# Convolution taps in S5: tables loaded six blocks ahead instead of three, and one more ScalarE copy per block

## The chip, the cores and the metric

The kernel runs on one core of one Trainium2 chip. The metric is the device time of one execution in microseconds (us). TensorE (PE) multiplies into PSUM banks, VectorE (DVE) and ScalarE (ACT) compute on SBUF and PSUM, SyncE (SP) issues nearly all DMAs of this kernel, each engine in the order of its own instruction list.

## What is computed

A two-layer encoder trunk on 512 tokens of width 2048. The change lies in layer 0, whose input projection feeds grouped-query attention and a bidirectional S5 layer:

```
h @ w_in -> q, k, v, g_a, u, g_b
o_a = gqa_block_attention(q, k, v) * silu(g_a)
o_b = s5_mixer(u, ...) * silu(g_b)      # scan of both directions, Re(C h) + D u, GLU
x   = x + gate * (concat([o_a, o_b]) @ w_out)
```

The kernel does S5 in blocks of eight tokens. A short convolution inside a block uses "taps" (products of C, powers of the state matrix, and B); a scan over the 64 blocks carries the state between blocks.

## The kernel before

Projections are units of float32 matmuls, each split into three (lines 167 to 169 with 512 columns, 234 to 236 with 256). Every weight piece of 128x1024 is loaded into a tile `w` (two buffers, L142), rounded by ACT into `wh` (L128) and subtracted by DVE into `wl` (L129); `wh` and `wl` have three buffers. Here "split" means the L129 instruction. In the stretch of interest the projection units use two PSUM banks in turn (`nmain = 2`).

A gate unit (ga0, ga1, ... of g_a) is emptied by `gate_evict`: ACT takes a tanh into the tile `r2k` (L890), DVE multiplies (L891), SP stores it (L892). `r2k` has one buffer, so the next L890 waits until the store before it has landed, and the bank of a unit is free only after its L891.

The S5 work is a background stream that runs between these units. After `s5_in` come, step by step together, `s5_scan` and `s5_kernels`; then comes `s5_out`.

- `s5_scan` is 62 steps on DVE alone, five instructions each (L483 twice, L484, L486 twice), each step needing the one before.
- `s5_kernels` makes the taps of 16 blocks. A block's table `ck` (512 KB) is read from the scratch tensor `s5_ck` (L414), 16 small matmuls (L521; the trace has two records for each) fill two banks, ACT copies them out (L528, L529), DVE adds to 16 columns (L530, and L532, which reads the second bank), SP stores the taps (L533). Three `ck` tiles are in use in turn, `G14` to `G16`, and `G17` holds the copied-out taps.
- `s5_out` reads the taps back in small pieces (L552), copies scan states (L559, L560: these need the whole scan), and multiplies (L570, L573).

The order on each engine is fixed when the program is built: a list scheduler places an instruction when its operands are ready, by its own estimate of time, and by priority, with weights first. On the chip each engine follows that order.

Of the kernel before, what the change touches and what calls it, by code (L numbers as in the profile page):

```python
# [13 lines left out]
ALU = mybir.AluOpType  # L14
# [52 lines left out]
class Trunk:  # L67
# [434 lines left out]
    def s5_kernels(self, ts):  # L502


        nc, A = self.nc, self.A
        self.s5_kk = self.scratch("s5_kk", [16, 128, 240])
        dd = self.sl("s5dd", [128, 2, 16])
        nc.sync.dma_start(out=dd[:, 0], in_=A["s5_dcol"])
        nc.sync.dma_start(out=dd[:, 1], in_=A["s5_dmask"])
        w = self.sl(ts[3], [128, 4, 240])  # L510
        cks = {i: self.s5_load_ck(ts[i], i) for i in range(3)}
        yield
        for i in range(16):
            ck = cks.pop(i)
            kv = [self.bank(f"b{2 * (i % 2) + d}", (128, 128)) for d in range(2)]
            for c in range(2):
                for g in range(4):
                    b0 = (i * 4 + g) // 2 * 32
                    for d in range(2):
                        r = slice(64 * d, 64 * d + 64)  # L520
                        nc.tensor.matmul(out=kv[d][32 * g:32 * g + 32], lhsT=self.s5_bb[c][r, b0:b0 + 32],  # L521
                                         rhs=ck[r, c, g], start=(c == 0), stop=(c == 1),
                                         tile_position=(64 * d, 32 * g))
            if i + 3 < 16:
                cks[i + 3] = self.s5_load_ck(ts[i % 3], i + 3)
            yield
            ks = w[:, i % 4]
            nc.scalar.copy(out=ks[:, 0:128], in_=kv[1])  # L528
            nc.scalar.copy(out=ks[:, 128:240], in_=kv[0][:, 16:128])  # L529
            nc.vector.scalar_tensor_tensor(out=ks[:, 112:128], in0=dd[:, 1], scalar=dd[:, 0, i:i + 1],  # L530
                                           in1=ks[:, 112:128], op0=ALU.mult, op1=ALU.add)
            nc.vector.tensor_tensor(out=ks[:, 112:128], in0=ks[:, 112:128], in1=kv[0][:, 0:16], op=ALU.add)  # L532
            nc.sync.dma_start(out=self.s5_kk[i], in_=ks)  # L533
            yield

# [389 lines left out]
    def layer0(self):  # L925
        nc, A = self.nc, self.A
        G = [f"G{i}" for i in range(18)]
# [144 lines left out]
        st = [t.rearrange("p (r g c) -> p r g c", r=2, g=32) for t in big]  # L1072
        ydram = self.scratch("ydram", [128, 64, 64])

        def s5_rest():
            yield from self.s5_in([G[14], G[3], G[1], G[2], G[15], G[16], G[17]], st)
            yield from self.qk_tables(("ropeq", "ropek"), G[8])
            a, b = self.s5_scan(st), self.s5_kernels(G[14:18])
            la = lb = True
            while la or lb:  # L1080
                la = la and next(a, "end") != "end"
                lb = lb and next(b, "end") != "end"
                yield
            yield from self.s5_out([G[14], G[15], G[3], G[16], G[10], G[17], G[11], G[0], G[2], G[1]], st, ydram)
        self.start("s5", s5_rest())
        self.sstep = SSLOT
        extra(17)
# [48 lines left out]
        for j in range(8):  # L1136
# [3 lines left out]
            w = self.sl((G[8], G[4], G[13])[j % 3], [128, 2, 512])  # L1140
# [839 lines left out]
```

## Time and profile before

| | |
|---|---|
| median of 3 runs | 1838.96 us (1835.25 to 1839.21) |
| profiled execution | 1831.32 us, of which the span is 1829.5 us |
| PE busy | 1770.3 us, 97% of the span |
| DVE busy | 1209.7 us, 66% |
| ACT busy | 730.0 us, 40% |
| DMA | 347.52 MB, 190 GB/s on average |

Busy shares are averages over stages with different limits. A busy PE is the sum of overlapping matmul records, so the pace of matmuls is read from the distance of their starts. The profiled execution is 0.4% shorter than the median; a sum made in its times is carried to the median as a difference.

### The profile page before, as it was taken

Reading aid. Unit: us, or ns where it says so; the run is one execution under the profiler, and the core shown is the slowest. Engines: PE = TensorE matmul, PEld = TensorE weight load, DVE = VectorE, ACT = ScalarE, POOL = GpSimd, SP = SyncE. Lnnn points to the kernel's source line nnn. Section 1 sums busy time; section 2 is a strip of 40 time slices with the busy share of each in tenths; the row PEclk is TensorE's granted clock in tenths of the full one; section 3 lists DMA queues with packets and bytes.
Section 4 is the critical chain, followed back from the end, with each engine's and each line's share of the span. In section 5 each row is a group of like instructions: output and inputs, shape, how many; then the busy total and the mean of one; then the engine's idle time right before and its main releaser. Section 6 shows DMA issues by size and latency. Waiting matters only on the chain.

```text
span 1829.5 us, 28824 instructions
## 1 busy us (share of the span) xinstructions
PE 1770.3 (97%) x11176; PEld 1522.8 (83%) x11176; DVE 1209.7 (66%) x2336; ACT 730.0 (40%) x1357; POOL 25.1 (1%) x44
## 2 busy tenths in 40 slices
PE   6899999899999989999999999999999999999999
PEld 3677897699989867888878878878799999997887
DVE  6897697984699999842256676589974453644332
ACT  6333454236235434432243244356644343442211
POOL 0000000000000000011100000000000000000000
PEclk8999999999999989999999999999999999999999
DMA  9997626747989887664435743358533333243542
GB/s 325 375 340 278 186 79 220 241 124 247 313 315 295 285 283 259 209 207 140 138 108 161 246 142 117 104 169 250 165 105 115 110 99 102 93 141 100 180 140 90
DMA packets 140906, 347.52 MB, mean 190 GB/s; under 512 B 31488, under 2 KB 42656, under 8 KB 140768
## 3 DMA queue, kind: packets, MB, share of 16 engines
q1 hardware_dynamic: 140768, 345.67, 57.6%
q8 instruction: 88, 1.44, 0.3%
q14 instruction: 50, 0.41, 0.1%
HBM read 310.48 MB, written 33.56 MB: 188 GB/s over the span
## 4 chain that ended last, share of the span: by engine, by line
PE 65%; DVE 16%; DMA 12%; issue 3%; ACT 1%; SPq 1%; DVEq 0%; ACTq 0%
PE m L167 10%; PE m L169 10%; PE m L168 10%; PE m L235 7%; PE m L234 7%; PE m L236 7%; DMA G<-in_ada_r_dram 6%; DVE G L629 3%; DVE wl L129 3%; PE b L169 2%; PE b L167 2%; PE b L168 2%; PE b L573 1%; PE b L973 1%; PE b L461 1%
## 5 line engine op out<-in xcount | busy, mean ns | idle before, releaser
L129 DVE TENSOR_TENSOR wl<-w,wh 128x1024 fp32r<-128x1024 f32 (+2 forms) x262 | 313.9, 1199 | 256.8 <-ACT wh L128 254.0
L128 ACT CAST wh<-w 128x1024 fp32r<-128x1024 f32 (+2 forms) x262 | 269.1, 1029 | 522.3 <-PE m L168 267.5
L168 PE MATMUL m<-H,wh 128*128 128x512 f32 (+1 forms) x968 | 381.9, 395 | 1.2 <-DVE H L992 1.2
L167 PE MATMUL m<-H,wh 128*128 128x512 f32 (+1 forms) x968 | 380.8, 398 | 2.2 <-ACT G L1144 2.1
L169 PE MATMUL m<-H,wl 128*128 128x512 f32 (+1 forms) x968 | 378.8, 396 | 2.2 <-DVE wl L129 2.2
L234 PE MATMUL m<-wh,H 128*128 128x256 f32 (+2 forms) x1232 | 353.3, 288 | 2.6 <-ACT H L665 1.5
L236 PE MATMUL m<-wh,H 128*128 128x256 f32 (+2 forms) x1232 | 353.8, 289 | 0.3 <-DVE H L1765 0.3
L235 PE MATMUL m<-wl,H 128*128 128x256 f32 (+2 forms) x1232 | 353.0, 287 | 0.2 <-DVE wl L129 0.2
L234 PEld LDWEIGHTS m<-wh,H 128*128 128x128 f32 x1232 | 233.8, 190 | 7.3 <-ACT H L665 2.6
L236 PEld LDWEIGHTS m<-wh,H 128*128 128x128 f32 x1232 | 233.4, 190 | 3.5 <-issue 1.0
L235 PEld LDWEIGHTS m<-wl,H 128*128 128x128 f32 x1232 | 234.0, 190 | 2.6 <-issue 0.7
L167 PEld LDWEIGHTS m<-H,wh 128*128 128x128 f32 x968 | 182.9, 190 | 46.0 <-issue 4.2
L169 PEld LDWEIGHTS m<-H,wl 128*128 128x128 f32 x968 | 181.8, 188 | 44.1 <-issue 3.5
L168 PEld LDWEIGHTS m<-H,wh 128*128 128x128 f32 x968 | 182.3, 188 | 42.4 <-issue 2.6
L629 DVE SCALAR_TENSOR_TENSOR G<-G,cb 128x1024 f32<-128x1024 f32 x128 | 155.0, 1220 | 55.5 <-DMA G<-in_ada_r_dram 47.7
L169 PE MATMUL m<-OLa,wl 128*128 128x512 f32 (+1 forms) x132 | 51.3, 389 | 0.6 <-DVE wl L129 0.5
L167 PE MATMUL m<-OLa,wh 128*128 128x512 f32 (+1 forms) x132 | 51.5, 390 | 0.2 <-ACT wh L128 0.2
L167 PE MATMUL m<-OLb,wh 128*128 128x512 f32 (+1 forms) x132 | 50.1, 388 | 1.4 <-ACT OLb L128 1.4
L167 PE MATMUL b<-H,wh 128*128 128x512 f32 x128 | 50.2, 406 | 0.8 <-DVE G L1045 0.8
L169 PE MATMUL m<-OLb,wl 128*128 128x512 f32 (+1 forms) x132 | 50.9, 386 | 0.0
L168 PE MATMUL m<-OLa,wh 128*128 128x512 f32 (+1 forms) x132 | 50.8, 385 | 0.0
L168 PE MATMUL m<-OLb,wh 128*128 128x512 f32 (+1 forms) x132 | 50.7, 384 | 0.0
(406 smaller groups left out, 2685.2 us busy)
## 6 DMA issues: line engine op xcount, KB each, us to landing
G<-in_ada_r_dram SPq DMA_DIRECT2D x128, 512.0 KB
w<-in_w_kvq_dram SPq DMA_DIRECT2D x72, 512.0 KB
w<-in_w_out_dram SPq DMA_DIRECT2D x64, 512.0 KB
w<-in_w_x_dram SPq DMA_DIRECT2D x36, 512.0 KB
OLa<-in_ada_dram SPq DMA_DIRECT2D x32, 512.0 KB
OLb<-in_ada_dram SPq DMA_DIRECT2D x32, 512.0 KB
G<-s_ck SPq DMA_DIRECT2D x32, 512.0 KB
s_ck<-G SPq DMA_DIRECT2D x16, 512.0 KB
```

The lines of the kernel that those rows point to most:

```text
L128: self.nc.scalar.copy(out=hi, in_=src)
L129: self.nc.vector.tensor_tensor(out=lo, in0=src, in1=hi.bitcast(F32), op=ALU.subtract)
L167: mm(out=out, lhsT=lh, rhs=rh, start=start, stop=False)
L168: mm(out=out, lhsT=lh, rhs=rl, start=False, stop=False)
L169: mm(out=out, lhsT=ll, rhs=rh, start=False, stop=stop)
L234: mm(out=o, lhsT=hi, rhs=wh[:, c], start=(k == 0 and i % per == 0), stop=False)
L235: mm(out=o, lhsT=hi, rhs=wl[:, c], start=False, stop=False)
L236: mm(out=o, lhsT=lo, rhs=wh[:, c], start=False, stop=last)
L461: nc.tensor.matmul(out=xp[c][:, gg * 64:gg * 64 + 64], lhsT=gt[:, c, g], rhs=self.s5_u(b * 4 + g))
L573: nc.tensor.matmul(out=yp[:, cols], lhsT=ck[:, c, g], rhs=sts[:, j % 2, c, g], start=False, stop=(c == 1))
L629: nc.vector.scalar_tensor_tensor(out=t, in0=t, scalar=1.0, in1=cb, op0=ALU.mult, op1=ALU.mult, accum_out=o)
L973: nc.tensor.matmul(out=ps[32 * i:32 * i + 32, 0:256], lhsT=self.cs[:, 4 * q + i:4 * q + i + 1].to_broadcast([128, 32]), rhs=abuf[k][:, q, ...
```

## The change

`s5_kernels` takes seven tiles instead of four: `ck` tables of six blocks are held in `G14`, `G15`, `G16`, `G1`, `G2`, `G3`, and the taps stay in `G17`, whose rows become 256 wide. A third ACT copy per block takes the 16 columns that DVE used to read from the bank into `k0`, so that DVE no longer reads PSUM there. Nothing else in the source changes.

```diff
-        w = self.sl(ts[3], [128, 4, 240])
-        cks = {i: self.s5_load_ck(ts[i], i) for i in range(3)}
+        w = self.sl(ts[6], [128, 4, 256])
+        k0 = w[:, :, 240:256]
+        cks = {i: self.s5_load_ck(ts[i], i) for i in range(6)}
...
-            if i + 3 < 16:
-                cks[i + 3] = self.s5_load_ck(ts[i % 3], i + 3)
-            yield
-            ks = w[:, i % 4]
+            if i + 6 < 16:
+                cks[i + 6] = self.s5_load_ck(ts[i % 6], i + 6)
+            yield
+            ks = w[:, i % 4, 0:240]
             nc.scalar.copy(out=ks[:, 0:128], in_=kv[1])
             nc.scalar.copy(out=ks[:, 128:240], in_=kv[0][:, 16:128])
+            nc.scalar.copy(out=k0[:, i % 4], in_=kv[0][:, 0:16])
...
-            nc.vector.tensor_tensor(out=ks[:, 112:128], in0=ks[:, 112:128], in1=kv[0][:, 0:16], op=ALU.add)
+            nc.vector.tensor_tensor(out=ks[:, 112:128], in0=ks[:, 112:128], in1=k0[:, i % 4], op=ALU.add)
...
-            a, b = self.s5_scan(st), self.s5_kernels(G[14:18])
+            a, b = self.s5_scan(st), self.s5_kernels(G[14:17] + G[1:4] + G[17:18])
```

The list scheduler places other instructions anew as well. In the rows below line numbers behind the change are higher by one or two (L890 to L892 are now L892 to L894, L570 and L573 are L572 and L575); the text keeps the old ones.

**SP, the store of ga0.** SP's list, before, from the third-last load of a `ck` table on. `w_2804` is the first weight piece of ga3, `w_2929` its second, `ga<-r2k_2668` the store of ga0.

```order
L414 DMA G_500_3351<-s_ck 128x1024
L142 DMA w_2804<-in_w_ga_dram 128x1024
L414 DMA G_503_3408<-s_ck 128x1024
L892 DMA ga<-r2k_2668 128x512
L533 DMA s_kk<-G_445_2706 128x240 x2
L414 DMA G_513_3490<-s_ck 128x1024
```

SP's list, of the change, from the second weight piece of ga3 (`w_2938`) on. `w_3060`, `w_3187` and `w_3309` are the first three pieces of k and v; the stores are of ga0, ga1, ga2.

```order
L142 DMA w_2938<-in_w_ga_dram 128x1024
L554 DMA G_531_3780<-s_kk 128x1x128 x7
L554 DMA G_538_3878<-s_kk 128x1x128
L142 DMA w_3060<-in_w_kvq_dram 128x1024
L554 DMA G_538_3878<-s_kk 128x1x128 x7
L142 DMA w_3187<-in_w_kvq_dram 128x1024
L894 DMA ga<-r2k_2668 128x512
L142 DMA w_3309<-in_w_kvq_dram 128x1024
L894 DMA ga<-r2k_2929 128x512
L894 DMA ga<-r2k_3178 128x512
```

The store of ga0 now stands behind three more weight loads and behind the tap reads of `s5_out`.

**ACT, the eviction of ga1.** ACT's list, before: the casts of weight pieces and the tanh of ga1 (`m_439`), ga2 (`m_465`) and ga3 (`m_485`). `wh_3045` and `wh_3170` are the two pieces of ga3, `wh_2925` the second piece of ga2.

```order
L128 CAST wh_2925<-w_2677 128x1024
L529 COPY G_445_2706<-b_521_3671 128x112
L528 COPY G_445_2706<-b_522_3672 128x128
L128 CAST wh_3045<-w_2804 128x1024
L890 ACTIVATE r2k_2920<-m_439_2672 128x512
L128 CAST wh_3170<-w_2929 128x1024
L128 CAST wh_3290<-w_3049 128x1024
L128 CAST wh_3417<-w_3174 128x1024
L890 ACTIVATE r2k_3165<-m_465_2924 128x512
L128 CAST wh_3559<-w_3294 128x1024
L890 ACTIVATE r2k_3410<-m_485_3169 128x512
```

ACT's list, of the change. ga2 is now `m_468`, ga3 `m_488`; `wh_2934` is the second piece of ga2, the next two are those of ga3, `wh_3305` the first of k.

```order
L531 COPY G_445_2706<-b_521_3686 128x16
L128 CAST wh_2934<-w_2677 128x1024
L128 CAST wh_3056<-w_2811 128x1024
L128 CAST wh_3183<-w_2938 128x1024
L128 CAST wh_3305<-w_3060 128x1024
L892 ACTIVATE r2k_2929<-m_439_2672 128x512
L892 ACTIVATE r2k_3178<-m_468_2933 128x512
L128 CAST wh_3430<-w_3187 128x1024
L128 CAST wh_3572<-w_3309 128x1024
L892 ACTIVATE r2k_3423<-m_488_3182 128x512
```

The tanh of ga1 moved behind two more casts, and that of ga2 stands right behind it. On DVE the multiply of ga1 (L891) stood behind 33 steps of the scan and stands behind 39 now; that of ga2 went from 43 to 42, that of ga3 from 46 to 50.

**PE, the start of `s5_out`.** PE's list, before, up to the first L573. `m_541` and `m_542` are the two banks of v, `wh_3880` its second weight piece.

```order
L234 MATMUL m_542_3879<-wh_3880,H_131_748 128x256
L235 MATMUL m_542_3879<-wl_3881,H_131_748 128x256
L236 MATMUL m_542_3879<-wh_3880,H_132_753 128x256
L234 MATMUL m_542_3879<-wh_3880,H_131_748 128x256
L235 MATMUL m_542_3879<-wl_3881,H_131_748 128x256
L236 MATMUL m_542_3879<-wh_3880,H_132_753 128x256
L573 MATMUL b_535_3803<-G_526_3748,G_527_3749 128x64 x2
```

PE's list, of the change, up to the same instruction (`wh_3896` is the second piece of v).

```order
L234 MATMUL m_541_3894<-wh_3787,H_82_408 128x256
L235 MATMUL m_541_3894<-wl_3788,H_82_408 128x256
L236 MATMUL m_541_3894<-wh_3787,H_83_413 128x256
L234 MATMUL m_541_3894<-wh_3896,H_89_468 128x256
L235 MATMUL m_541_3894<-wl_3897,H_89_468 128x256
L236 MATMUL m_541_3894<-wh_3896,H_90_473 128x256
L575 MATMUL b_535_3819<-G_526_3764,G_527_3765 128x64 x2
```

From the first L521 to the first L573 PE's list had 223 projection matmuls of 512 columns and 288 of 256; now it has 223 and 219. The last L521 stood behind 112 of them and stands behind 86 now. DVE's list had 14 splits inside the scan and has 13; ahead of the end of the first head pair of attention it had 38 instructions of the stream L629 and has 45.

## Rows read from the trace of the kernel before

**Rows 1.** The page's first line.

```profile
span 1829.5 us, 28824 instructions
```

**Rows 2.** Waits from 285 to 400 us: us in total, times, longest.

```profile
PE b L521 <- DMA G<-s_ck: 7.4, 6, 1.7
...
ACT r2k L890 <- DMA ga<-r2k: 4.4, 1, 4.4
...
PE m L234 <- DVE r2k L891: 1.1, 1, 1.1
```

**Rows 3.** Stretches of 10 us: busy times, clock, DMA share, GB/s.

```profile
305.00:315.00 10.00, 7.54 (x111) 5.06 (x111) 9.76 (x38) 2.28 (x7) 0.00 (x0) 1.00 0.80 256
```

**Rows 4.** DVE's timeline: start, duration, instruction, idle time before.

```profile
294.99 0.38 DVE L483 TENSOR_TENSOR w2k<-OLb,s5lt 128x128 f32<-128x128 f32 x1 [7.87 <-ACT OLb L469]
...
300.14 0.38 DVE L483 TENSOR_TENSOR w2k<-OLa,s5lt 128x128 f32<-128x128 f32 x1
...
301.55 0.38 DVE L483 TENSOR_TENSOR w2k<-OLa,s5lt 128x128 f32<-128x128 f32 x1
...
307.59 0.68 DVE L891 SCALAR_TENSOR_TENSOR r2k<-r2k,m 128x512 f32<-128x512 f32 x1
...
340.61 1.22 DVE L129 TENSOR_TENSOR wl<-w,wh 128x1024 fp32r<-128x1024 f32 x1
341.75 0.28 DVE L486 TENSOR_TENSOR OLa<-OLa,w2k 128x64 f32<-128x64 f32 x1
...
402.11 0.28 DVE L486 TENSOR_TENSOR OLb<-OLb,w2k 128x64 f32<-128x64 f32 x1
```

**Rows 5.** The chain that ended last: start, us, what.

```profile
362.29 4.95 DMA ga<-r2k
...
403.60 0.66 PE b L573 x4
```

**Rows 6.** ACT's timeline.

```profile
340.99 0.25 ACT L529 COPY G<-b 128x112 f32<-128x112 f32 x1 [1.68 <-issue]
...
367.32 0.60 ACT L890 ACTIVATE r2k<-m 128x512 f32<-128x512 f32 x1 [4.41 <-DMA ga<-r2k]
...
402.29 0.62 ACT L559 COPY G<-OLa 64x512 f32<-64x512 f32 x1 [2.41 <-DVE OLa L486]
402.93 0.62 ACT L560 COPY G<-OLa 64x512 f32<-64x512 f32 x1
```

**Rows 7.** PE's timeline: a block of L521, and 512-column matmuls.

```profile
340.19 0.67 PE L521 MATMUL b<-G,G 64*32 64x128 f32 x32
340.80 0.50 PE L167 MATMUL m<-H,wh 128*128 128x512 f32 x1
...
341.36 0.40 PE L169 MATMUL m<-H,wl 128*128 128x512 f32 x1
...
345.97 0.39 PE L168 MATMUL m<-H,wh 128*128 128x512 f32 x1
```

**Rows 8.** Line 234 from 340 to 405 us: count, ns min/median/max, first and last start.

```profile
L234 PE MATMUL m<-wh,H x96: 278/283/384, 368.7 to 403.1; 128*128 128x256 f32 x96
```

**Rows 9.** SP's timeline.

```profile
361.27 0.33 SPq L142 DMA_DIRECT2D w<-in_w_kvq_dram  x1
...
362.29 0.45 SPq L892 DMA_DIRECT2D ga<-r2k  x1
```

**Rows 10.** Stretches of 50 us: columns as in group 3.

```profile
650.00:700.00 50.00, 41.63 (x200) 33.87 (x199) 46.98 (x100) 19.51 (x47) 0.00 (x0) 0.90 0.84 281
700.00:750.00 50.00, 48.42 (x248) 40.50 (x247) 47.60 (x97) 24.07 (x41) 0.14 (x2) 1.00 0.75 236
```

**Rows 11.** PE's timeline behind a wait in attention.

```profile
680.49 0.58 PE L168 MATMUL b<-OLb,G 128*128 128x256 f32 x1 [4.37 <-DVE OLb L129]
...
681.51 0.41 PE L169 MATMUL b<-OLb,G 128*128 128x256 f32 x1
...
681.73 0.41 PE L167 MATMUL b<-OLb,G 128*128 128x256 f32 x1
...
684.27 0.40 PE L167 MATMUL b<-G,G 128*128 128x512 f32 x1
```

## The prediction, made before the changed kernel was run

> **What bounds the kernel now.** I read the page first, then the waits and the 10-us stretches around `s5_kernels`, then the timelines of DVE, SP, ACT and PE there. The profiled execution has a span of 1829.5 us [rows 1] and took 1831.32 us; the median is 7.6 us longer, so the sum gives a difference that is added to the median.
>
> Two engines run side by side here. DVE has the scan: its first real step starts at 294.99, the last ends at 402.11 + 0.28 = 402.4 us [rows 4], and it is 9.76 of 10 us busy between [rows 3]. PE has the blocks of taps and fills the rest with projections. It waits six times for a `ck` table, 7.4 us in total [rows 2]; in the worst stretch it is 7.54 of 10 us busy [rows 3]. That is the wait which the change goes for. But the next thing after the taps, the first L573 of `s5_out`, starts at 403.60 [rows 5], 1.2 us behind the end of the scan and right behind the copies L559 and L560 [rows 6]. So the scan ends last, on DVE, and PE's projections ahead of it are filler: what PE gains there is worth something only if it does more of them before 403.60. The order does the opposite: 69 projection matmuls of 256 columns fewer stand ahead of the first L573.
>
> **What the change costs, step by step.**
>
> *Loads.* The number of `ck` loads is the same; those of blocks 3 to 5 are issued earlier. If all six waits vanish PE gains 7.4 us at 340 us; if the DMA queues, 80% busy at 256 GB/s [rows 3], are as late as now, nothing. Both ends are kept, but below a later wait swallows either.
>
> *The extra copies.* 16 copies of 16 columns, which no row shows, cost between nothing and the 0.25 us of a 112-column copy [rows 6], 4.0 us at most. ACT is 2.28 of 10 us busy [rows 3] and waits for PE and DMA, so they lie in idle time and I take 0; uncovered they would be 4.0. L532 now reads SBUF: between nothing and the 0.28 us of a 64-column L486 [rows 4], where DVE is the bound at most 16 x 0.28 = 4.5 us either way. I take no change, since it is as small a piece of work as before.
>
> *The new place of the gate evictions.* This is the large term. Prices: a scan step 1.41 us (300.14 to 301.55), a split 1.14 (340.61 to 341.75), a gate multiply 0.68 [rows 4]; a 512-column matmul 0.23 (20 from 341.36 to 345.97) [rows 7], a 256-column one 0.121 (96 triples from 368.7 to 403.1) [rows 8]; a store from issue to landing 4.95 [rows 5], the issue 0.4 [rows 9], a tanh 0.60 [rows 6]. Test on the order before: 295.0 + 62 x 1.41 + 14 x 1.14 + 5 x 0.68 = 401.8, against 402.4 measured. Now the new order, with the places counted in DVE's list:
>
> 1. The split of ga3's second piece stands behind 36 steps, 6 splits and 2 multiplies: 295.0 + 50.8 + 6.8 + 1.4 = 354.0, done at 355.1. Only then is the buffer free for the weight load that now stands ahead of the store of ga0. The store is issued by 355.5 and lands at 360.5.
> 2. `r2k` has one buffer, so the tanh of ga1 runs to 361.1. DVE has reached its multiply (39 steps, 8 splits, 2 multiplies: 360.5) and is done at 361.8. Only then is the bank free in which PE must start ga3.
> 3. PE would start ga3 much earlier: the split of ga2's second piece is done at 295.0 + 29 x 1.41 + 4 x 1.14 + 2 x 0.68 + 1.14 = 343.0, 24 matmuls later it is 348.5. So PE waits 13.3 us in one piece. Whatever the loads gave is spent here.
> 4. PE then does the 47 matmuls of ga3 by 372.6. Meanwhile the store of ga1 lands at 361.8 + 0.4 + 4.95 = 367.1, the tanh of ga2 ends at 367.7; DVE, three steps on at 366.0, waits 1.7 us and finishes the multiply at 368.4.
> 5. The multiply of ga3 is 8 steps and 2 splits further, 382.0 to 382.7. Its own inputs are there by 374.3 (store of ga2 landed at 373.7, tanh). PE has done the first 24 matmuls of k at 375.5 and needs that bank: it waits 7.2 us.
> 6. Behind 382.7 PE has 168 matmuls of k and 27 of v, 195 x 0.121 = 23.6 us: it reaches L573 at 406.3. The scan has 12 steps and 3 splits left and ends at 403.0, the copies 1.2 us later. So L573 starts at 406.3 instead of 403.6, **2.7 us late**, and PE has 69 x 0.121 = **8.3 us** of projections left over: 11.0 us behind in all.
>
> Such a wait existed before too, but small: ACT 4.4 us for `ga<-r2k`, PE 1.1 for a multiply [rows 2], with the store issued at 362.29 behind a weight load [rows 9].
>
> *What is given back.* `s5_out` then takes its time as before plus 6 more matmuls (102 of them lie in it instead of 96), 0.7 us; so the stream L629 and attention, which follow it on DVE, start 3.4 us late, PE 11.0. From 650 to 750 us PE has idle time, 50 - 41.63 + 50 - 48.42 = 10.0 us, at a DVE that is 94% and 95% busy [rows 10]: there DVE sets the end. If DVE sets it wholly, the delay is 3.4; if PE does, 11.0. DVE's list now does 45 instead of 38 of L629 ahead of the first head pair, so part of its work is moved into the time in which it waits for PE. I take the middle, **+7.2 us**. Behind 750 us PE is the bound and the order is nearly the same, so the rest is carried through. Profiled execution 1838.5, median 1838.96 + 7.2 = **1846.2 us**.
>
> One rule speaks for the other sign, and rows for a repeating gap are there: the waits for `ck` come six times at up to 1.7 us [rows 2]. The Trainium skill, "Perfetto Trace Analysis", section "Identifying Performance Opportunities", says that a gap which repeats on the engine that should be saturated can mean too few buffers for the next tile. By that rule more `ck` tiles would remove 7.4 us and the time would be 1831.6. This trace bears it out as to the cause (the gaps end with a load), but not as to what ends last, which is the scan.
>
> **Rivals.** A change of 0.2%, 3.7 us, is about what a measurement of this kernel can tell from none.
>
> - *Faster.* The repeating gap closes and nothing takes its place on the way to 403.6, or the leftover projections fall wholly into PE's idle 10.0 us. For it speak [rows 2, 10]. It needs the store of ga0 to land before some 347 us, where PE wants the bank; the order puts it behind a split that DVE reaches at 354.0. Price: the whole 7.4 us, 1831.6 us. Chance 0.12.
> - *The same.* The delay is real at 406 us but DVE sets the end of attention and hides all but its own 3.4 us, or gains that back because L629 is further ahead: 1838.96 + 0 to 3.4, say 1841. Chance 0.18. The change failing to do what it says (tables still late at 256 GB/s) ends in the forecast, since the gate evictions set PE's pace either way.
> - *Slower, the forecast.* 1846, with its own range 1842.7 to 1854. Its upper part: behind a wait of 4.37 us the granted clock was down, 0.90 over 650 to 700 us [rows 10]; matmuls of 256 columns then came every 0.22 us, which is the lower of its two levels, 1.2 GHz, until the one at 684.27 [rows 11]. That is 3.8 us at half pace, 1.9 us lost, and the two new waits are longer. The first loss is hidden in the second wait, the second is not: 11.0 + 1.9 = 12.9 us, 1852, and some 2 us more if the stores land later. Chance 0.70.
>
> The range 1835.5 to 1854 leaves out most of the faster case and the far end of the slower one. Faster by over 0.2%: 0.12, same 0.18, slower 0.70.
>
> **What would show it.** Right, if the waits for `s_ck` on L521 shrink from 7.4 us to under 3; if PE then waits near 348 to 362 and near 375 to 383 us, put down to the multiply on `r2k` or to a store; if ACT's tanh of ga1 waits for `ga<-r2k`; if the first L573 starts between 403 and 408 us, and the v unit still has matmuls left when `s5_out` ends. Steps 1 to 6 are wrong if PE arrives at L573 ahead of the scan and waits there for L560: then only the 8.3 us of leftover projections remain. The give-back is wrong if PE's idle time from 650 to 750 us stays near 10 us, or vanishes altogether. The forecast fails as a whole if the store of ga0 is not behind that weight load in time, or if the reordered attention is itself more than 4 us better.

## The result, and the profile after

The changed kernel took 1856.28 us (median of 4 runs, 1850.72 to 1857.88) against 1837.11 us for the kernel before (4 runs). The medians differ by 19.2 us; the ratio is 1.0107, 95% interval 1.0085 to 1.0129, which is 19.7 us slower (15.6 to 23.7). A repeat (e19_after_again, below) gave 1854.67 against 1835.74 us, ratio 1.0101 (1.0087 to 1.0116). The forecast was 1846.2, or +7.2 us: the sign was right, the size far too small, and the time lies above the range. Two runs far above all others, 4572.77 us (e9) and 6155.35 us (the kernel before, beside e12 to e15), enter no ratio and no median below.

The profiled execution took 1855.67 us. Its page begins:

```profile
span 1853.9 us, 28823 instructions
```

The waits of PE and ACT in the change between 285 and 403 us (us in total, times, longest), to be held against [rows 2]:

```profile
PE m L167 <- DVE r2k L893: 7.7, 1, 7.7
PE b L522 <- ACT G L531: 3.4, 1, 3.4
PE b L572 <- DMA G<-s_kk: 3.0, 1, 3.0
...
PE b L575 <- ACT G L562: 0.5, 1, 0.5
PE m L234 <- DVE r2k L893: 0.4, 1, 0.4
PE b L522 <- DMA G<-s_ck: 0.2, 1, 0.2
...
ACT G L530 <- DMA s_kk<-G: 18.5, 6, 6.6
...
ACT r2k L892 <- DMA ga<-r2k: 4.8, 1, 4.8
```

The change did what it says: the wait for tables fell from 7.4 to 0.2 us. In its place stand one wait of 7.7 us for a gate's multiply on `r2k`, one of 3.4 for the new last copy of a block, and one of 3.0 for the first tap that `s5_out` reads back. ACT's copies of taps (L530) also wait, 18.5 us in all, for a store to free one of the four slots in `G17`. The timelines of SP, ACT and PE show the chain that the prediction named (start, duration, instruction, idle time before it):

```profile
354.39 0.49 SPq L894 DMA_DIRECT2D ga<-r2k  x1
...
358.77 0.60 ACT L892 ACTIVATE r2k<-m 128x512 f32<-128x512 f32 x1 [4.80 <-DMA ga<-r2k]
...
360.85 0.80 PE L167 MATMUL m<-H,wh 128*128 128x512 f32 x1 [7.74 <-DVE r2k L893]
361.44 0.63 PE L168 MATMUL m<-H,wh 128*128 128x512 f32 x1
...
363.58 0.55 PE L167 MATMUL m<-H,wh 128*128 128x512 f32 x1
363.97 0.39 PE L168 MATMUL m<-H,wh 128*128 128x512 f32 x1
364.19 0.39 PE L169 MATMUL m<-H,wl 128*128 128x512 f32 x1
```

The store leaves at 354.39, the tanh behind it starts at 358.77, and PE goes on at 360.85. Its next matmuls start some 0.43 us apart and only from 363.97 on 0.23 us apart, the lower and the upper of the clock's two levels (1.2 and 2.4 GHz); the granted clock is 0.66 from 355 to 365 us.

Two lines mark the ends of the stretches: the last multiply of `s5_out`, and the first matmul that sums squares behind the output projection (operation, count, duration, first and last start). The kernel before:

```profile
L573 PE MATMUL b<-G,G x256: 217/275/323, 403.6 to 457.8; 128*128 128x64 f32 x128
...
L1189 PE MATMUL b<-r2k,ones x4: 377/378/379, 934.1 to 934.7; 128*128 128x256 f32 x4
```

The change:

```profile
L575 PE MATMUL b<-G,G x256: 217/275/323, 401.1 to 456.0; 128*128 128x64 f32 x128
...
L1191 PE MATMUL b<-r2k,ones x4: 377/378/379, 953.6 to 954.3; 128*128 128x256 f32 x4
```

The repeat of the change (e19_after_again):

```profile
L575 PE MATMUL b<-G,G x256: 217/275/323, 403.9 to 458.7; 128*128 128x64 f32 x128
...
L1191 PE MATMUL b<-r2k,ones x4: 377/379/380, 959.9 to 960.5; 128*128 128x256 f32 x4
```

`s5_out` is not late; it ends 1.8 us earlier. Of that, 1.3 us is not the change's: the scan's first real step started at 293.70 instead of 294.99 [rows 4], and in the repeat at 296.34 with `s5_out` ending at 458.7. Counted from that step, `s5_out` ends after 162.8 us before and 162.3 and 162.4 in the change. So the S5 work costs nothing, and 8.3 us of projections (69 matmuls of 256 columns) are left over. But from there to the sums of squares the kernel before needs 934.1 - 457.8 = 476.3 us and the change 953.6 - 456.0 = 497.6: 21.3 us more, 13.0 beyond the leftover. That is attention. One execution is too little to size it, though. In e2, e3, e4 and e11 below, where PE, DVE and ACT have the order of the kernel before throughout this stretch, it takes 479.8, 482.9, 478.7 and 480.4 us, and in the repeat of the change 501.2. By the means, 479.6 in five executions and 499.4 in two, the change needs 19.8 us more, 11.5 beyond the leftover. The stretches that answer to [rows 10]:

```profile
650.00:700.00 50.00, 37.18 (x167) 30.04 (x166) 45.85 (x100) 19.80 (x49) 0.00 (x0) 0.81 0.81 263
700.00:750.00 50.00, 44.07 (x226) 37.71 (x225) 47.23 (x107) 23.15 (x42) 0.14 (x2) 0.91 0.65 206
```

PE's idle time there grew from 10.0 to 18.8 us, and the granted clock fell from 0.90 and 1.00 to 0.81 and 0.91. PE's largest waits from 457 to 770 us:

```profile
PE b L741 <- DVE G L732: 5.9, 1, 5.9
PE b L167 <- ACT G L841: 5.1, 1, 5.1
PE b L823 <- DVE G L129: 3.4, 1, 3.4
PE m L169 <- DVE wl L129: 2.9, 1, 2.9
```

DVE's timeline shows what stood ahead of the second of them, and PE's when it went on (L631 is the stream that was L629; L838 is the maximum of a softmax row, L839 its scaling, L841 ACT's exponential):

```profile
688.88 0.20 DVE L839 TENSOR_SCALAR sst<-sst,rq 128x1 f32<-128x1 f32 x1
691.78 1.23 DVE L631 SCALAR_TENSOR_TENSOR G<-G,cb 128x1024 f32<-128x1024 f32 x1 [2.70 <-DMA cb<-cbd]
692.93 0.08 DVE L631 DVE_READ_ACCUMULATOR G<-G,cb 128x1 f32 x1
692.93 0.69 DVE L838 TENSOR_REDUCE sst<-b 128x1 f32<-128x512 f32 x1
693.54 1.21 DVE L631 SCALAR_TENSOR_TENSOR G<-G,cb 128x1024 f32<-128x1024 f32 x1
...
694.68 1.22 DVE L631 SCALAR_TENSOR_TENSOR G<-G,cb 128x1024 f32<-128x1024 f32 x1
...
697.18 0.19 DVE L839 TENSOR_SCALAR sst<-sst,rq 128x1 f32<-128x1 f32 x1
...
697.46 0.78 ACT L841 ACTIVATE G<-b,sst,rq 128x512 f32<-128x512 f32 x1 [4.66 <-DVE sst L839]
...
698.38 0.79 PE L167 MATMUL b<-G,G 128*128 128x512 f32 x1 [5.14 <-ACT G L841]
```

An L631 at the head of DVE's list waits 2.70 us for the load of its broadcast operand `cb`, and everything behind it waits too. That one and two more L631 stand ahead of the L839 on which ACT's exponential and, 1.2 us later, PE depend. Before, PE's largest wait here was 4.37 us [rows 11].

### The profile page after: what moved, and what is told of

The parts are those of the page before. It is cut to its first block, busy times and chain, and to the rows that moved or that the text cites. A ratio compares the mean times of both kernels' runs of the same rounds, so it can differ in the third digit from the quotient of the medians.

```text
span 1853.9 us, 28823 instructions
## 1 busy us (share of the span) xinstructions
PE 1778.1 (96%) x11176; PEld 1531.6 (83%) x11176; DVE 1210.7 (65%) x2336; ACT 730.9 (39%) x1373; POOL 25.4 (1%) x44
## 4 chain that ended last, share of the span: by engine, by line
PE 70%; DVE 15%; DMA 9%; issue 3%; ACT 2%; SPq 0%; DVEq 0%; ACTq 0%
PE m L167 11%; PE m L168 11%; PE m L169 11%; PE m L234 7%; PE m L235 7%; PE m L236 7%; DMA G<-in_ada_r_dram 4%; PE b L169 2%; PE b L167 2%; PE b L168 2%; DVE wl L129 2%; DVE w2k L483 2%; PE b L575 1%; DVE G L631 1%; PE b L975 1%
## 5 line engine op out<-in xcount | busy, mean ns | idle before, releaser
L234 PE MATMUL m<-wh,H 128*128 128x256 f32 (+2 forms) x1232 | 353.1, 287 | 1.6 <-ACT H L667 1.2
L631 DVE SCALAR_TENSOR_TENSOR G<-G,cb 128x1024 f32<-128x1024 f32 x128 | 154.9, 1219 | 67.2 <-DMA G<-in_ada_r_dram 56.9
```

The lines of the kernel that those rows point to most:

```text
L234: mm(out=o, lhsT=hi, rhs=wh[:, c], start=(k == 0 and i % per == 0), stop=False)
L631: nc.vector.scalar_tensor_tensor(out=t, in0=t, scalar=1.0, in1=cb, op0=ALU.mult, op1=ALU.mult, accum_out=o)
```

## The experiments

Differences are the recorded ratios applied to the median of the kernel before on the same chip, with 95% intervals; a stretch read from a trace is one execution. Theory A: late gate stores leave projections behind `s5_out`, and attention, placed anew, loses more. Rival B: the tables and their loads cost it. Rival C: the third copy does. In the listings `...` marks what is left out.

**Which part of the change.** The six tables alone (the third copy and `k0` taken out):

```diff
-        k0 = w[:, :, 240:256]
...
-            nc.scalar.copy(out=k0[:, i % 4], in_=kv[0][:, 0:16])
...
-            nc.vector.tensor_tensor(out=ks[:, 112:128], in0=ks[:, 112:128], in1=k0[:, i % 4], op=ALU.add)
+            nc.vector.tensor_tensor(out=ks[:, 112:128], in0=ks[:, 112:128], in1=kv[0][:, 0:16], op=ALU.add)
```

> The six tables alone, without the third ScalarE copy; VectorE reads the bank again. In its order 278 projection matmuls of 256 columns stand ahead of the first L573 (288 before, 219 in the change), and the L629 instructions ahead of the first four head pairs are 38, 51, 74, 83 (before 38, 47, 71, 80; change 45, 59, 79, 86). Theory A (the loss comes from the late gate stores, which leave projections behind s5_out and have attention placed anew): 1.2 us left over and attention half way between the two orders, so +2 to +10 us against before. Rival B (the loss comes from the tables, their earlier loads and what these collide with): as slow as the change, +15 us or more.

Measured 1846.06 against 1834.32 us, ratio 1.0062 (1.0045 to 1.0079), +11.4 us: just above what A allowed, below B's bound. Little is left over here (278 of the 288 projections stand ahead of the first multiply of `s5_out`, which ends at 458.7), yet the stretch to the sums of squares (944.2) takes 485.5 us, 5.9 above the mean of the order of before, in one execution. So attention seems to lose time without PE being late by much.

The third copy alone, with three tables (`w` 256 wide, `k0`, and the copy, in the kernel before):

> The third ScalarE copy alone, with three tables. Its order behind S5 is that of before on every engine. Theory A: within 0.2% of before (-3 to +3 us), since 16 copies of some 0.2 us lie in idle time of ScalarE and VectorE saves nothing that it could use. Rival C (the copies themselves are the loss, by the longer wait of a bank for ScalarE): +5 us or more.

Measured 1834.21, ratio 0.9995 (0.9981 to 1.0009). The copies cost nothing that shows; C falls.

**Undoing the wait.** The whole change, with ga0 to ga3 evicted into two halves of `G13` in turn:

```diff
+        self.gt_tile(G[13])
         for j in GA0:
             self.tunit(self.h_rhs, 16, self.gate_evict(ga[j]))
+        self.gt = lambda: self.sl("r2k", [128, 512])
```

> The whole change, and the gates ga0 to ga3 are emptied into the two halves of G13 in turn, instead of the one r2k tile. The order then has 288 matmuls ahead of the first L573 as before, and on every engine the order behind S5 is that of before. Theory A: the loss vanishes; PE saves most of the 7.4 us of waits for tables, the scan still sets the start of s5_out at some 402 us, so 0 to -6 us against before. Rival B (tables or copies are the loss): it stays +15 us or more, since both are in it unchanged.

Measured 1834.65, ratio 1.0004 (0.9992 to 1.0017). The loss is gone, with all six tables and all copies in place, which speaks against B. In its trace PE waits 0.7 us for a gate's multiply instead of 8.1. The two ends of the stretch:

```profile
L575 PE MATMUL b<-G,G x256: 217/275/323, 403.7 to 457.8; 128*128 128x64 f32 x128
...
L1193 PE MATMUL b<-r2k,ones x4: 378/378/379, 940.7 to 941.3; 128*128 128x256 f32 x4
```

The whole change with eight staging slots for the taps instead of four:

```diff
-        w = self.sl(ts[6], [128, 4, 256])
-        k0 = w[:, :, 240:256]
+        ws = [self.sl(t, [128, 4, 256]) for t in ts[6:8]]
...
-            ks = w[:, i % 4, 0:240]
+            w = ws[i // 4 % 2]
+            ks, k0 = w[:, i % 4, 0:240], w[:, :, 240:256]
...
-            a, b = self.s5_scan(st), self.s5_kernels(G[14:17] + G[1:4] + G[17:18])
+            a, b = self.s5_scan(st), self.s5_kernels(G[14:17] + G[1:4] + G[17:18] + G[0:1])
```

> The whole change, and the taps are staged in eight slots (G17 and G0) instead of four, so that ScalarE need not wait for the store of the block four before (18.5 us in six waits in the profile of the change). r2k stays single. The order has 288 matmuls ahead of the first L573 and attention as before. Theory A: 0 to -6 us against before, as e3, with the waits of ScalarE for s_kk under 3 us. Rival B: +15 us or more.

Measured 1833.74, ratio 0.9994 (0.9981 to 1.0007). Either mend alone gives back the time, and in the trace the order of before on PE, DVE and ACT from the end of `s5_out` to the sums of squares. So the single `r2k` and the four slots bring the loss about together, and these two runs do not tell a wait on the chip from what the scheduler made of it. The prediction did not see the slots (ACT's 18.5 us).

**Both mends together.**

> The whole change with both mends: ga0 to ga3 evicted into two halves of G13 in turn, and eight staging slots for the taps (G17 and G0). The order of PE from the k and v units on is that of before, as in e3_gate2 and e4_slots8. Theory A: the scan on DVE, which ends at 402.4 us, still sets the first L573, so nothing is gained by PE's saved waits: -2 to +2 us. Rival (the table waits are worth something once no other wait takes their place): -4 to -7 us, with the first L573 before 400 us.

Measured 1834.07, ratio 0.9998 (0.9983 to 1.0013), with the first multiply of `s5_out` at 402.3. Nothing is gained, but this does not price the waits for tables by themselves: PE's waits from 285 to 403 us are 9.6 us, 3.8 of them for tables and 5.8 for taps, against 9.0 before. That the scan ends last is read from its distance: the first multiply starts 108.6 us behind the scan's first real step before, 107.4 in the change and 108.2 here.

**Being late, by itself.** The kernel before, with 29 matmuls of 512 columns in ga4's bank ahead of its first own one:

```diff
+            for _ in range(dummy if p == 0 else 0):
+                self.nc.tensor.matmul(out=ps, lhsT=wh[:, 0:128], rhs=rhs(0)[0], start=True, stop=True)
...
-            self.tunit(self.h_rhs, 16, self.gate_evict(ga[j]))
+            self.tunit(self.h_rhs, 16, self.gate_evict(ga[j]), 29 if j == GAK[0] else 0)
```

> The kernel before, with 29 additional matmuls of 512 columns (lhsT and rhs those of ga4's first matmul, overwritten by it) ahead of ga4, directly behind the last L573 of s5_out. Everything up to there, tables, copies, gate stores, keeps the order of before; PE is 29 x 0.23 = 6.7 us late for attention, as it is in the change (8.3 us of leftover projections less 1.8 us of an earlier end). The scheduler knows of the lateness and moves L629 ahead of the head pairs much as in the change (45, 59, 75, 83 instead of 38, 47, 71, 80). Theory A (being late makes the scheduler place attention anew, with L629 ahead of the softmax rows, and that order costs more than the lateness): +13 to +20 us, and PE's waits from 457 to 770 us grow from 10 to over 15 us. Rival P (a late PE costs at most what it is late, and the rest of the loss belongs to something else of the change): +3 to +7.5 us, and the waits stay at or below 11 us.

Measured 1842.32 against 1834.75, ratio 1.0045 (1.0027 to 1.0062), +8.3 us (5.0 to 11.4). A's +13 to +20 is missed; P's bound of 7.5 lies inside the interval. PE's waits from 457 to 770 us are 13.1 us, neither A's 15 nor P's 11. In the trace the stretch from `s5_out` to the sums of squares takes 487.3 us, 7.7 above the mean of the order of before, of which 6.7 are the added matmuls. So in this run lateness is passed on in full, where the prediction halved it, but it explains at most 8.3 of the change's 19 us.

**Holding L629 back.** In these kernels a piece of L629 may be placed only behind the output multiply of a given head pair; in e9 and e10 pieces from the 39th on are held this way (`hp[n]` is the output multiply of head pair n + 1). The core of it:

```diff
+HOLD = {38: 0, 47: 1, 71: 2, 80: 3}
...
+            n = max((HOLD[a] for a in HOLD if a <= i), default=None)
+            with nullcontext() if n is None else self.tc.issue_after(self.hp[n].ins):
+                nc.vector.scalar_tensor_tensor(out=t, in0=t, scalar=1.0, in1=cb, op0=ALU.mult, op1=ALU.mult, accum_out=o)
```

> As e8_late_pe, but L629 is held: pieces from the 39th on may come only behind the output multiply of head pair 1, from the 48th, 72nd and 81st behind those of pairs 2, 3 and 4, which gives 38, 47, 64, 75, 88, 97, 101, 104 pieces ahead of the eight pairs (before 38, 47, 71, 80, 96, 98, 102, 104). Theory A in the form that L629 ahead of the softmax is what costs: +4 to +9 us, about the 6.7 us of the added matmuls, and at least 6 less than e8_late_pe. Rival P: within 2 us of e8_late_pe. Third case: if e8_late_pe is over +13 and this one stays within 3 us of it, the cost lies in another part of the new order, or in being late at these places by itself.

> The whole change, its order up to the end of s5_out untouched (69 projections fewer ahead of the first L573, PE's wait for the gate's multiply), with L629 held as in e9_late_pe_held: 38, 47, 64, 79, 93, 99, 102, 104 pieces ahead of the pairs instead of 45, 59, 79, 86, 96, 96, 96, 99. Theory A in the form that L629 ahead of the softmax costs the second part: +5 to +10 us against before, where the change itself is +19. Rival P, or the cost in another part of the order: +16 to +21.

e9 measured 1838.59, ratio 1.0024 (1.0010 to 1.0038), +4.4 us: 3.9 less than e8 (uncertain by some 4), not the 6 that was expected. e10 measured 1843.51, ratio 1.0052 (1.0035 to 1.0068), +9.5 us, where the change has +19: half of the loss is gone with nothing changed up to the end of `s5_out`, and what is left is about the 8.3 us of leftover projections. PE's waits in the stretch that end with DVE fall from 13.4 to 2.0 us, all its waits from 20.2 to 14.5 (sums of that view's rows).

The same hold in e1 (first kernel), and only from pair 3 on in the whole change (second):

> The six tables without the third copy (as e1_tables, +11.4 us against before with only some 2 us of lateness at the end of s5_out), with L629 held: 38, 47, 67, 77, 91, 99, 102, 104 pieces ahead of the eight head pairs instead of 38, 51, 74, 83, 96, 97, 102, 104. Theory A (L629 ahead of the softmax and head preparation is what costs in attention): +1 to +5 us. Rival (the tables themselves, their six loads in a row or the later queue, cost it): +9 to +13 us.

> The whole change with L629 held only from head pair 3 on: 45, 59, 71, 80, 95, 98, 102, 104 pieces ahead of the eight pairs, where the change has 45, 59, 79, 86, 96, 96, 96, 99 and e10_after_held 38, 47, 64, 79, 93, 99, 102, 104. If the pieces ahead of pairs 3 and 4 are what costs (at 690 us, where PE's transposes wait for a softmax and a head preparation that stand behind four L631 in a row): +8 to +12 us, as e10_after_held. If those ahead of pairs 1 and 2 cost: +16 to +21, as the change. Between: both share it.

e12 measured 1841.69 against 1834.84, ratio 1.0038 (1.0020 to 1.0055), +7.0 us (3.7 to 10.1): better than e1's +11.4, but between the +1 to +5 of A and the +9 to +13 of its rival, so it decides for neither; PE waited for other instructions of DVE instead, 6.0 us for one softmax row. e16 measured 1850.09 against 1835.74, ratio 1.0080 (1.0062 to 1.0098), +14.7 us, between the cases: both halves of the pairs share it. The number of pieces ahead of a pair is no price by itself: e12 has no more of them ahead of the first four pairs than the kernel before (38, 47, 67, 77 against 38, 47, 71, 80) and is slower.

**Looking for a faster version.** The kernel before with L629 held from pair 3 on, the mended change with the same hold, and the kernel before held further:

> The kernel before, nothing else changed, with L629 held from pair 3 on: 38, 47, 64, 75, 88, 97, 101, 104 pieces instead of 38, 47, 71, 80, 96, 98, 102, 104. Theory A: faster by 1 to 5 us, since e9_late_pe_held, with 6.7 us of added matmuls, lost only 4.4; PE's waits from 457 to 770 us fall from 10 to under 6 us. Rival (e9 gained only what the added matmuls had moved, the order before is as good as any): within 1.5 us of before.

> The whole change with both mends (as e11_gate2_slots8, -0.3 us), L629 held as in e13_before_held. Theory A: the same as e13_before_held within 2 us, since the tables are worth nothing with the scan as the last to end. Rival: at least 3 us faster than e13_before_held.

> The kernel before with L629 held further: 32, 40, 56, 66, 80, 90, 97, 100 pieces ahead of the pairs, some 8 fewer than in e13_before_held from pair 3 on. If L629 ahead of the softmax costs in proportion, another 1 to 4 us are won; if the held work only comes back later, behind 750 us, where the weights' splits need DVE, it is 0 to 5 us slower than e13_before_held.

Measured 1835.37, 1835.07 and 1836.06 against 1834.84: ratios 1.0005 (0.9991 to 1.0018), 1.0004 (0.9990 to 1.0018) and 1.0010 (0.9997 to 1.0022). Nothing is won. In e15 PE is busy 47.51 of 50 us from 650 to 700, against 41.63 [rows 10], but 42.33 from 750 to 800, against 49.23: the held work comes back there.

**Without L629.** The last question was whether the loss in attention hangs on L629 at all. Both kernels with its 96 multiplies of layer 0 and the additions of their sums left out, the loads kept, and the change beside them:

> The kernel before with all 96 L629 of layer 0 left out (the conditioning columns of layer 0 are not added; their loads stay). Tells what DVE's 96 x 1.14 us or more in attention cost as a whole: faster by 3 to 12 us if DVE sets the end of attention, since PE's 11 us of waits and its time at the lower clock there go; no change (within 2 us) if it does not.

> The whole change with the same 96 L629 left out. The gate chain stays, and 54 projection matmuls (6.5 us) are left over behind s5_out. Theory A (the loss beyond the lateness comes from L629 ahead of the softmax): slower than e17_before_no_l629 by 4 to 10 us, the lateness alone. Rival (it hangs on another part of the new order): slower than it by 15 to 21 us.

> The change itself, beside the three others on the same chip, as their reference: +16 to +22 us against before.

e17 measured 1823.84 against 1835.74, ratio 0.9937 (0.9922 to 0.9953), -11.6 us. e18 measured 1826.56, ratio 0.9951 (0.9938 to 0.9965): 2.6 us above e17, with an uncertainty of some 4 us (both intervals together). That is just below the 4 to 10 that A allowed and far from its rival's 15 to 21. e19 stands at +18.5 beside them. The two ends of the stretch, in e17:

```profile
L573 PE MATMUL b<-G,G x256: 217/275/323, 409.3 to 463.4; 128*128 128x64 f32 x128
...
L1190 PE MATMUL b<-r2k,ones x4: 377/378/379, 922.4 to 923.1; 128*128 128x256 f32 x4
```

and in e18:

```profile
L575 PE MATMUL b<-G,G x256: 217/275/323, 411.6 to 466.6; 128*128 128x64 f32 x128
...
L1192 PE MATMUL b<-r2k,ones x4: 377/378/379, 932.0 to 932.6; 128*128 128x256 f32 x4
```

The stretch takes 459.0 and 465.4 us: 6.4 us more with the change, and the 54 projections left over in e18 are 54 x 0.121 = 6.5 us. PE has no wait between these two lines in either, and the granted clock is 1.00 throughout. The gate chain is still there: e18's PE waits 6.6 us for the gate's multiply. So without L629 the change costs what it leaves over, or less; with it, 19.8 us of the stretch by the means above. This does not show that the places of L629 are the whole of the rest: without its multiplies DVE is also no longer full (236.5 us busy in e17's stretch, 337.8 before), so that another fault of the new order could hide there.

## Why the prediction was wrong in size

- **What ends last in S5: right for the kernel before, wrong for the change.** The prediction had PE's projections end last in the change, at 406.3. PE came ahead of the scan instead and waited 0.5 us for the copy L562 (L560 before), the prediction's own sign that steps 1 to 6 are wrong; the scan sets the first multiply of `s5_out` before and after. The waits for tables went (7.4 to 0.2 us), and nothing was gained. The Trainium skill, "Perfetto Trace Analysis", section "Identifying Performance Opportunities", says that a gap which repeats on the engine that should be saturated can mean too few buffers. The trace agrees as to the cause: with six tables the gap closed. It was worth nothing here.
- **Copies at no cost: right** (e2).
- **Loads: right in the main, with a new wait missed.** PE reaches the first tap of `s5_out` before its read has landed (3.0 us), and ACT waits for the staging slots (18.5 us).
- **The gate chain, steps 1 and 2: right within 2 us.** The store leaves at 354.39 (forecast 355.5), PE goes on at 360.85 (361.8).
- **Step 3: too large.** The split came as forecast (done at 341.9, forecast 343.0), but PE was still busy with earlier work, behind waits of 3.4 us for a copy and 3.0 for a tap that the prediction did not have. It reached the bank at 353.1 instead of 348.5, so the wait was 7.7 instead of 13.3 us.
- **Steps 4 to 6: too large.** The second wait was 0.4 us instead of 7.2: PE came at 379.3, not at 375.5, and the multiply was done at 379.7, not 382.7. Nothing of these waits reached 401: there only the 8.3 us left over remained of the forecast 11.0.
- **"What is given back" is the step that failed.** It took the middle between 3.4 and 11.0 us, +7.2, because DVE sets part of the pace in attention, and it put the L629 moved ahead at no cost, as work moved into idle time. The opposite happened: beyond the 8.3 us left over, the new order of attention cost another 10 to 12 us (19.7 and 18.5 less 8.3 by the times, 11.5 by the traces), and PE's idle time from 650 to 750 us grew from 10.0 to 18.8 us. The row on which the step rested [rows 10] was read rightly, PE idle at a DVE that is 95% busy. What did not follow is that work moved earlier on DVE is free: the list is in order, and in the timeline above L631 stands ahead of a softmax row for which PE waits. The upper end of the range had no term for this either, only the clock's 1.9 us and later stores.
- **The halving of the lateness is not settled.** For 6.5 to 6.7 us of delay the times say 8.3 (5.0 to 11.4, e8), 4.4 (1.8 to 7.0, e9, L629 held) and 2.6 (uncertain by 4, e18 against e17). The traced stretches of e8 (+7.7) and e18 (+6.4) speak for all of it, that of e9 (482.0 us, +2.4) for less.

An account of the 19.8 us in the traces: 8.3 are projections left over; PE's waits between the two ends sum to 21.9 us (20.2 and 23.6) instead of 13.2 (11.0 to 14.4 in the five executions), which is 8.7; 2.8 are left, for which the rows show only the lower clock: over the stretch it falls short of full by 13.7 us in both executions instead of 5.1 to 8.5, in part while PE waits anyway. From the sums of squares to the end the span has another 895.4 to 897.6 us in the order of before and 900.3 and 897.2 in the change, which is too near to say anything.

Shown by experiments: that one `r2k` buffer and four slots together bring the loss about, by the order that follows from them (mending either gives back that of before and its time); that the third copy has no part; that no loss beyond the lateness shows without L629's multiplies; and that their places are worth about half of the loss (e10). Only argued, from the timeline: that the wait of one L631 for `cb`, with the softmax behind it, is part of what makes the change's places worse than those of e8. From 457 to 770 us DVE waits 6.8 us for `cb` in the change and 0.3 in e8, but also 4.3 before, 6.2 in e10 and 9.3 in e12, so this wait alone does not order the kernels by their loss. Which property of an order of L629 sets its price stays open, and with it why e12 keeps 7.0 us.

## What to carry to other kernels

A wait that repeats on the busiest engine is worth closing only if that engine ends last at the next joint; here another engine's chain did, and closing the wait gained nothing. Where a list scheduler sets the order, a change of buffers far ahead moves work on every list: count what stands ahead of the next joint, price what is left over in full until a run says otherwise, and look in the next stage for long, unhurried instructions that may have moved ahead of short urgent ones. PE's idle time beside a full DVE is no reserve that a delay can be booked against. And take the same order several times before sizing a stretch: five executions of one order gave 476.3 to 482.9 us here.

## What the runs showed of the hardware that was not expected

- The places of L629 act on the clock too. With L629 PE's granted clock is 0.90 and 1.00 [rows 10] or 0.81 and 0.91 from 650 to 750 us; in e17 and e18, without waits, it is 1.00 in all of attention. Without L629's 96 multiplies of 1.2 us the stretch takes 459.0 us (e17), with them 476.3 to 482.9 in the order of before. The scan's first real step came late in both kernels without them, at 301.10 us in e17 and 303.19 in e18 instead of 294.99, ahead of all these multiplies; the cause stays open, and it may be why the median of e17 fell by less.
- A DVE instruction that waited 2.70 us for a load held up everything behind it in DVE's list: DVE ran nothing from 689.08 to 691.78 us.
- Executions differ ahead of the change's place: the first real step of the scan began at 293.70 and 296.34 us in two executions of one kernel. Ends were therefore compared from that step on.
